# Parking only the sums' two parts in the down projections, with twelve parked and nine summed pairs per layer

## The chip, the cores and the metric

The kernel runs on one core of a Trainium2 chip. The metric is the device time of one execution in microseconds (us). TensorE is called PE here (PEld its weight loads), VectorE DVE, ScalarE ACT, GpSimd POOL and SyncE SP.

## The reference

Two post-norm layers on an input of 256 positions by 2048 features, all in 32-bit floats. Layer 0 mixes tokens with a gated MLP, layer 1 with latent attention; each mixer is followed by the same kind of gated MLP with a short convolution, and it is this MLP's last product that the change touches:

```python
def conv_ffn(x, w_up, conv_w, conv_b, w_down):
    h = x @ w_up                     # 2048 -> 2 * 5504
    ...                              # causal convolution of width 3 along the positions
    a, g = jnp.split(h, 2, axis=-1)
    return (jax.nn.silu(g) * a) @ w_down      # 5504 -> 2048: the down projection
...
    f = conv_ffn(x, ffn_w_up[i], ffn_conv_w[i], ffn_conv_b[i], ffn_w_down[i])
    x = layer_norm(ALPHA * x + f, ln_ffn_g[i], ln_ffn_b[i])
```

## The kernel before

**Products in parts.** PE multiplies a rounded type (`F32R`). So each operand is split into a high part `hi`, which ACT casts (line 125), and a low part `lo` = operand - `hi`, which DVE subtracts (line 128). A product is then three matmuls: high by high, low by high, high by low (`prod_b`).

**Units.** The down projection takes its 43 blocks of 128 rows of `w_down` in pairs, called units here (0 to 21; unit 21 is a single block). It does so twice, once for each half of the 2048 output columns, upwards in the first half and downwards in the second. A weight chunk of a unit is 128 partitions by 2 blocks of 1024 columns, thus 2048 columns in four pieces of 512. Each unit is of one of three kinds, written down by hand in `PLAN`:

- `e`, wide: `Banks.eight`, 8 products of 128 x 128 by 128 x 512, so 24 matmuls. The weights need two `big` tiles (high and low part).
- `s`, summed ("seven"): `Banks.seven`, 7 products, 21 matmuls, in the manner of Strassen's scheme. `_seven` forms four sums of the pieces (lines 135 and 138) and splits both the last three pieces (`wh`, `wl`, 1536 columns) and the sums (`th`, `tl`, 2048 columns). It takes five `big` tiles, one of which (`ts`, the sums themselves) is free once they are split. The activations need sums as well: `turn` (four small DVE instructions), two casts and two subtractions in `Acts.make`, in a room of their own, while two wide units share a room.
- `p`, parked: also 7 products, but the four tiles `wh`, `wl`, `th`, `tl` were made earlier, while the up projection ran, and stored in DRAM (`park`); `fetch` brings them back on POOL's DMA queue into four `side` tiles.

**Feeding.** `Feed` hands out the chunks in order. Before PE's work on a unit is issued, `next` has the following two (near the end three) split and two more loaded; `fetch` is called up to five units ahead (`LEAD`). Loads go through SP's queue, parking and fetching through POOL's. The tiles come from three pools of slots:

```python
SLOTS = {"big": 14, "raw": 3, "side": 6}
```

`raw` holds loaded weights until they are split, `big` split weights, activations, up to two residual tiles and four of the six tiles that hold the up projection's result (`act`), `side` the parked parts, the other two `act` tiles, and some activations of the second half. An instruction whose tile has no free slot waits until the users of an older tile are done.

**Parking.** `park` is a generator. `park_all` runs through the parked units in order, and the up projection takes one step of it (`next(jobs, None)`) behind two of the four chunks of most of its groups, 38 places in all. A parked unit takes four steps: load; split of the three plain pieces and two stores; the four additions; split of the sums and two stores.

**Ends.** After the last summed or parked unit of a half, `rest` and `fold` (DVE) take the banks of its sums into the residual; at the end of a half `piece` takes the other banks. The last three units (four in layer 1) are done bank by bank, interleaved with the layer norm.

The order of instructions on each engine follows from the program's order and the tiles' dependencies, arranged when the program is built.

Of the kernel before, what the change touches and what calls it, by code (L numbers as in the profile page):

```python
# [8 lines left out]
F32 = mybir.dt.float32  # L9
F32R = mybir.dt.float32r  # L10
BF16 = mybir.dt.bfloat16
AF = mybir.ActivationFunctionType
ALU = mybir.AluOpType
AX = mybir.AxisListType

P = 128
# [7 lines left out]
NF_FF = DFF // P  # L24
# [31 lines left out]
SLOTS = {"big": 14, "raw": 3, "side": 6}  # L56
# [4 lines left out]

PLAN = {NF_GM: ("0e 1e 2s 3e 4e 5s 6e 7e 8s 9e 10e 11s 12e 13e 14s 15e 16e 17s 18e 19e 20s 21e 22e 23e",
                "23e 22e 21e 20s 19e 18e 17s 16e 15e 14s 13e 12e 11s 10e 9e 8s 7e 6e 5s 4e 3e 2e 1e 0e"),
        NF_FF: ("0e 1p 2e 3s 4e 5e 6p 7e 8s 9e 10e 11p 12e 13s 14e 15p 16e 17s 18e 19s 20e 21e",
                "21e 20e 19p 18e 17s 16e 15p 14e 13s 12e 11p 10s 9e 8s 7p 6e 5s 4e 3e 2e 1e 0e")}
KINDS = {"e": "wide", "s": "seven", "p": "parked"}
FIRST = ((19, 1), (20, 0), (20, 2))
LEAD = 5
# [8 lines left out]
class Feed:  # L77
# [3 lines left out]
    def __init__(self, nc, pin, behind, order, pool, dram, chunks):  # L81
        self.pin, self.behind, self.order, self.sums = pin, behind, order, None
        self.nc, self.pool, self.dram, self.chunks = nc, pool, dram, chunks
        self.kept = {}
        self.raw, self.parts = {}, {}
        self.loaded = self.split = self.used = 0

    def _load(self):
        ap, cols, kind = self.chunks[self.loaded][:3]
        if kind == "parked":  # L90
            self.fetch(self.loaded)
            self.loaded += 1
            return
        t = self.pool.tile([P, 2048], F32, tag="raw", name=f"raw{self.loaded}", bufs=SLOTS["raw"])
        if len(ap.shape) == 3:
            self.behind(self.nc.sync.dma_start(t.rearrange("p (k c) -> p k c", k=ap.shape[1]), ap))
        else:
            step = 1024 if self.loaded < 3 else cols
            for o in range(0, cols, step):
                self.behind(self.nc.sync.dma_start(t[:, o : o + step], ap[:, o : o + step]))  # L100
        self.raw[self.loaded] = t
        self.loaded += 1

    def _split(self):
        i = self.split
        cols, kind = self.chunks[i][1:3]
        if kind == "parked":
            self.split += 1
            return
        raw = self.raw.pop(i)  # L110
        if kind == "seven":
            self.parts[i] = self._seven(i, raw)
            self.split += 1
            return
        hi = self.pool.tile([P, 2048], F32R, tag="big", name=f"wh{i}", bufs=SLOTS["big"])
        lo = self.pool.tile([P, 2048], F32R, tag="big", name=f"wl{i}", bufs=SLOTS["big"])
        step = 512 if i == 0 else cols if kind == "wide" and i > 2 else 1024 if cols == 2048 else cols // 2
        for o in range(0, cols, step):
            c = slice(o, o + step)
            self._cast(hi[:, c], lo[:, c], raw[:, c])  # L120
        self.parts[i] = (hi, lo)
        self.split += 1

    def _cast(self, hi, lo, raw):
# [23 lines left out]
    def park(self, i):  # L148

        nc, pin = self.nc, self.pin  # L150
        tile = lambda n, dt: self.pool.tile([P, 2048], dt, tag="side", name=f"{n}{i}", bufs=SLOTS["side"])
        add = lambda o, a, b: pin(nc.vector.tensor_tensor(o, a, b, ALU.add))
        self.kept[i] = kept = {}

        def store(n, t, cols):
            d = self.dram.tile([P, cols], F32, tag=f"kept{n}{i}", name=f"kept{n}{i}", bufs=1)
            pin(nc.gpsimd.dma_start(d, t[:, 0:cols].bitcast(F32)))
            kept[n] = d

        ap = self.chunks[i][0]  # L160
        raw = tile("praw", F32)
        pin(nc.gpsimd.dma_start(raw.rearrange("p (k c) -> p k c", k=ap.shape[1]), ap))
        yield
        for n, o, cols in (("w", 512, 1536), ("t", 0, 2048)):
            hi, lo = tile(f"p{n}h", F32R), tile(f"p{n}l", F32R)
            pin(nc.scalar.copy(hi[:, 0:cols], raw[:, o : o + cols]))
            pin(nc.vector.tensor_tensor(lo[:, 0:cols], raw[:, o : o + cols], hi[:, 0:cols].bitcast(F32), ALU.subtract))
            store(f"{n}h", hi, cols)
            store(f"{n}l", lo, cols)
            if n == "w":  # L170
                yield
                r = [raw[:, 512 * i : 512 * (i + 1)] for i in range(4)]
                add(r[1], r[1], r[0])
                add(r[0], r[0], r[2])
                add(r[2], r[2], r[1])
                add(r[3], r[3], r[2])
                yield

    def fetch(self, i):

        if i in self.parts:
            return
        got = self.parts[i] = []
        for n in ("wh", "wl", "th", "tl"):
            d = self.kept[i].pop(n)
            t = self.pool.tile([P, 2048], F32R, tag="side", name=f"f{n}{i}", bufs=SLOTS["side"])
            self.behind(self.nc.gpsimd.dma_start(t[:, 0 : d.shape[1]], d))
            got.append(t)
# [9 lines left out]
    def next(self, splits=2, loads=2):  # L198
        i = self.used
        self.ahead(i + 1 + splits + loads, i + 1 + splits)  # L200
        self.used += 1
        got = self.parts.pop(i)
        near = [j for j in range(i + 1, min(i + 1 + LEAD, len(self.chunks))) if self.chunks[j][2] == "parked"]
        if near and near[0] in self.kept:
            self.fetch(near[0])
        return got
# [3 lines left out]
def trunk(ctx: ExitStack, tc: tile.TileContext, x, xT, gm_in, gm_wout, ffn_up, ffn_dn,  # L210
# [344 lines left out]
    def boundary(ln, acc, end, tag, after):  # L555
# [15 lines left out]
        ln.piece(1, fs[1], acc[1][fs[1]])  # L571
        g = group(ln, tag)
        next(g)
        ln.put(0, 2)
        ln.scale(0, 3)
        ln.put(0, 3)
        ln.start(1)
        ln.scale(1, 0)
        next(g)
        ln.scale(1, 1)  # L580
        next(g)
        ln.put(1, 0)
        ln.scale(1, 2)
# [768 lines left out]
```

## Time and profile before

| | us |
|---|---|
| median of three runs | 2465.78 (2465.09 to 2467.02) |
| span of the profiled execution | 2464.6 |
| up projection and its boundary, layer 0 (780.0 to 1271.5) | 491.5 |
| down projection, layer 0 (1271.5 to 1493.9) | 222.4 |
| down projection, layer 1 (2232.2 to 2454.7) | 222.5 |
| last instructions behind it (2455.0 to 2464.6) | 9.6 |

The profile is of one execution on the chip. Its span runs from the first to the last instruction; the times of the runs hold a little more than that. A "busy" engine has an instruction in flight; matmuls overlap one another, so the time that one takes of PE is the distance between two starts, not its duration. A row of a group tells count, busy time, mean duration in ns of one, and the idle time ahead of it with what ended it. A row of the timeline tells start, duration, engine, line, what is written and read, and in brackets the engine's idle time just before and what ended it. Numbers of buffers are left out of tile names: `wh` is any unit's high part.

### The profile page before, as it was taken

What the parts mean: (1) busy time and instruction counts of PE and PEld (TensorE: products, weight loads), DVE (VectorE), ACT (ScalarE), POOL (GpSimd) and SP (SyncE); (2) the same over time, 40 slices, a digit from 0 to 9 for tenths busy, and PEclk for the clock granted to TensorE, in tenths of its full rate; (3) what the DMA queues carried; (4) which work ended last, traced back from release to release, by engine and by line L of the source; (5) the groups of instructions that cost most, each with busy time, mean ns of one, the idle gap of its engine ahead of it and who ended that gap; (6) DMA issues with size and microseconds to landing.
All of it is one profiled execution on the core that took longest, in us unless ns stands there. A gap on an engine that the chain in (4) does not pass through costs nothing. (4 is left out here: it accounts for less than half of the span.)

```text
span 2464.6 us, 32483 instructions
## 1 busy us (share of the span) xinstructions
PE 2458.1 (100%) x12494; PEld 2091.3 (85%) x12494; DVE 2054.7 (83%) x2734; ACT 1459.3 (59%) x1967; POOL 104.2 (4%) x202
## 2 busy tenths in 40 slices
PE   9999999999999999999999999999999999999999
PEld 7888888888888888888888888988888888888887
DVE  7999999989897788778777997867598787878798
ACT  6666665566565666656554566665565665555453
POOL 0000000000000000000001000000000000000000
PEclk9999999999999999999999999999999999999999
DMA  7555666656665778778868885544478787777885
GB/s 291 202 208 205 226 204 202 205 188 205 222 212 198 241 282 314 300 279 300 322 218 318 301 301 182 184 170 156 172 269 309 275 305 304 295 265 278 299 324 201
DMA packets 116428, 611.94 MB, mean 248 GB/s; under 512 B 10648, under 2 KB 10912, under 8 KB 75184
## 3 DMA queue, kind: packets, MB, share of 16 engines
q1 hardware_dynamic: 90128, 462.47, 52.9%
q0 software_dynamic: 26144, 147.39, 15.8%
q8 instruction: 98, 1.61, 0.3%
q14 instruction: 58, 0.48, 0.1%
HBM read 544.75 MB, written 65.06 MB: 247 GB/s over the span
## 5 line engine op out<-in xcount | busy, mean ns | idle before, releaser
L128 DVE TENSOR_TENSOR wl<-raw,wh 128x1024 fp32r<-128x1024 f32 (+4 forms) x645 | 958.4, 1501 | 169.5 <-ACT wh L125 124.0
L125 ACT CAST wh<-raw 128x1024 fp32r<-128x1024 f32 (+4 forms) x645 | 809.0, 1278 | 356.8 <-PE up L230 80.7
L230 PE MATMUL up<-xhl,wh 128*128 128x512 f32 x2624 | 611.4, 390 | 0.0
L230 PEld LDWEIGHTS up<-xhl,wh 128*128 128x128 f32 x2624 | 487.4, 188 | 97.8
L230 PEld LDWEIGHTS up<-xhl,wl 128*128 128x128 f32 x2624 | 325.8, 192 | 6.4
L230 PE MATMUL up<-xhl,wl 128*128 128x256 f32 x2624 | 328.1, 283 | 0.0
L125 ACT CAST th<-ts 128x1536 fp32r<-128x1536 f32 (+1 forms) x138 | 142.5, 1052 | 110.9 <-DVE ts L135 80.3
L230 PE MATMUL ub<-wh,xhl 128*128 128x512 f32 x576 | 179.5, 393 | 0.0
L128 DVE TENSOR_TENSOR tl<-ts,th 128x1536 fp32r<-128x1536 f32 (+1 forms) x138 | 163.2, 1221 | 10.4 <-PE dn_p L230 3.4
L230 PEld LDWEIGHTS ub<-wh,xhl 128*128 128x128 f32 x576 | 108.1, 188 | 24.2 <-issue 1.9
L230 PE MATMUL ub<-wl,xhl 128*128 128x512 f32 x288 | 112.1, 389 | 0.0
L135 DVE TENSOR_TENSOR ts<-ts,raw 128x512 f32<-128x512 f32 x138 | 95.1, 689 | 1.4
L135 DVE TENSOR_TENSOR ts<-raw 128x1024 f32<-128x1024 f32 x69 | 84.3, 1221 | 6.1 <-PE ub L230 3.8
L230 PE MATMUL mo<-wh,oT 128*128 128x512 f32 x256 | 82.5, 401 | 0.0
L230 PE MATMUL v_q<-wh,xhl 128*128 128x512 f32 x224 | 70.7, 391 | 0.3 <-ACT wh L125 0.3
L230 PEld LDWEIGHTS ub<-wl,xhl 128*128 128x128 f32 x288 | 54.1, 188 | 11.3
L230 PE MATMUL v_p<-wh,xhl 128*128 128x512 f32 x192 | 59.9, 389 | 0.0
L230 PEld LDWEIGHTS mo<-wh,oT 128*128 128x128 f32 x256 | 45.5, 189 | 7.1
L230 PEld LDWEIGHTS v_q<-wh,xhl 128*128 128x128 f32 x224 | 42.0, 188 | 10.5 <-ACT wh L125 1.9
L230 PE MATMUL mo<-wl,oT 128*128 128x512 f32 x128 | 50.1, 391 | 0.0
L724 ACT ACTIVATE lny<-lnt,lncol 128x128 f32<-128x128 f32 x96 | 36.6, 472 | 15.6 <-PE lnt L720 15.5
L388 DVE TENSOR_TENSOR h_0a<-up,lo_0a 128x256 f32<-128x256 f32 x41 | 17.2, 421 | 33.0 <-ACT lo_0a L386 33.0
(1838 smaller groups left out, 4338.4 us busy)
## 6 DMA issues: line engine op xcount, KB each, us to landing
raw<-in_ffn_up_dram SPq DMA_DIRECT2D x172, 1024.0 KB, 7.0
raw<-in_gm_in_dram SPq DMA_DIRECT2D x93, 1024.0 KB, 5.3
raw<-in_ffn_dn_dram SPq DMA_DIRECT2D x68, 1024.0 KB, 7.2
raw<-in_gm_wout_dram SPq DMA_DIRECT2D x48, 1024.0 KB, 5.3
praw<-in_ffn_dn_dram POOLq DMA_DIRECT2D x16, 1024.0 KB, 13.9
keptth<-pth POOLq DMA_DIRECT2D x16, 1024.0 KB, 8.1
kepttl<-ptl POOLq DMA_DIRECT2D x16, 1024.0 KB, 8.8
fth<-keptth POOLq DMA_DIRECT2D x16, 1024.0 KB, 9.4
```

The lines of the kernel that those rows point to most:

```text
L125: cast = self.nc.scalar.copy(hi, raw)
L128: self.nc.vector.tensor_tensor(lo, raw, hi.bitcast(F32), ALU.subtract)
L135: add = lambda o, a, b: self.nc.vector.tensor_tensor(o, a, b, ALU.add)
L230: recent[0] = nc.tensor.matmul(o, l, r, start=start, stop=stop, skip_group_check=True)
L388: nc.vector.tensor_tensor(h, acc[:, 0:S], lo, ALU.add)
L724: nc.scalar.activation(y[:, j], t[:, j * P : (j + 1) * P], AF.Identity, bias=lncol[:, o : o + 1], scale=lncol[:, g : g + 1])
```

## The change

A parked unit no longer stores and fetches the parts of its three plain pieces. `park` has three steps now: load, the four additions, and the split of the sums with two stores. `fetch` brings back two tiles instead of four. The plain pieces are loaded into a `raw` tile on SP's queue when the unit's turn comes, in two DMAs (512 columns and 1024 columns), and split like a wide unit's, 1536 columns at once, into two `big` tiles. `next` looks for the next parked unit that is not fetched yet.

`PLAN` changes for both layers' down projections: from eight parked and ten summed units per layer to twelve and nine, so 21 units of 7 products instead of 18. The plan of the gated MLP's output (`NF_GM`) stays.

```diff
-        NF_FF: ("0e 1p 2e 3s 4e 5e 6p 7e 8s 9e 10e 11p 12e 13s 14e 15p 16e 17s 18e 19s 20e 21e",
-                "21e 20e 19p 18e 17s 16e 15p 14e 13s 12e 11p 10s 9e 8s 7p 6e 5s 4e 3e 2e 1e 0e")}
+        NF_FF: ("0e 1p 2e 3s 4e 5p 6s 7e 8p 9e 10s 11e 12p 13s 14e 15p 16e 17s 18e 19p 20e 21e",
+                "21e 20e 19p 18s 17e 16p 15e 14s 13p 12e 11s 10p 9e 8p 7s 6e 5p 4e 3e 2e 1e 0e")}
...
     def _load(self):
         ap, cols, kind = self.chunks[self.loaded][:3]
+        t = self.pool.tile([P, 2048], F32, tag="raw", name=f"raw{self.loaded}", bufs=SLOTS["raw"])
         if kind == "parked":
+            self.behind(self.nc.sync.dma_start(t[:, 0:512], ap[:, 0, 512:1024]))
+            self.behind(self.nc.sync.dma_start(t[:, 512:1536], ap[:, 1]))
             self.fetch(self.loaded)
-            self.loaded += 1
-            return
...
     def _split(self):
...
-        if kind == "parked":
-            self.split += 1
-            return
...
+        cols = 1536 if kind == "parked" else cols
...
-        self.parts[i] = (hi, lo)
+        self.parts[i] = (hi, lo, *self.fetched.pop(i, ()))
...
     def park(self, i):
...
-        for n, o, cols in (("w", 512, 1536), ("t", 0, 2048)):
...
+        add(r[1], r[1], r[0])
+        add(r[0], r[0], r[2])
+        add(r[2], r[2], r[1])
+        add(r[3], r[3], r[2])
+        yield
+        hi, lo = tile("pth", F32R), tile("ptl", F32R)
+        pin(nc.scalar.copy(hi, raw))
+        pin(nc.vector.tensor_tensor(lo, raw, hi.bitcast(F32), ALU.subtract))
+        store("th", hi, 2048)
+        store("tl", lo, 2048)
...
     def fetch(self, i):
...
-        for n in ("wh", "wl", "th", "tl"):
+        for n in ("th", "tl"):
```

More of the change, by code (lines that the diff above doesn't have):

```diff
@@ L83, in __init__ @@
         self.nc, self.pool, self.dram, self.chunks = nc, pool, dram, chunks
-        self.kept = {}
+        self.kept, self.fetched = {}, {}
         self.raw, self.parts = {}, {}
@@ L89, in _load @@
         ap, cols, kind = self.chunks[self.loaded][:3]
+        t = self.pool.tile([P, 2048], F32, tag="raw", name=f"raw{self.loaded}", bufs=SLOTS["raw"])
         if kind == "parked":
+            self.behind(self.nc.sync.dma_start(t[:, 0:512], ap[:, 0, 512:1024]))
+            self.behind(self.nc.sync.dma_start(t[:, 512:1536], ap[:, 1]))
             self.fetch(self.loaded)
-            self.loaded += 1
-            return
-        t = self.pool.tile([P, 2048], F32, tag="raw", name=f"raw{self.loaded}", bufs=SLOTS["raw"])
-        if len(ap.shape) == 3:
+        elif len(ap.shape) == 3:
             self.behind(self.nc.sync.dma_start(t.rearrange("p (k c) -> p k c", k=ap.shape[1]), ap))
@@ L116, in _split @@
         lo = self.pool.tile([P, 2048], F32R, tag="big", name=f"wl{i}", bufs=SLOTS["big"])
-        step = 512 if i == 0 else cols if kind == "wide" and i > 2 else 1024 if cols == 2048 else cols // 2
+        cols = 1536 if kind == "parked" else cols
+        step = 512 if i == 0 else cols if kind == "parked" else cols if kind == "wide" and i > 2 else 1024 if cols == 2048 else cols // 2
         for o in range(0, cols, step):
@@ L163, in park @@
         yield
-        for n, o, cols in (("w", 512, 1536), ("t", 0, 2048)):
[L165 to L177, printed above, removed]
+        r = [raw[:, 512 * i : 512 * (i + 1)] for i in range(4)]
+        add(r[1], r[1], r[0])
[8 more added lines that the diff above has]
+        store("tl", lo, 2048)
     def fetch(self, i):
-        if i in self.parts:
+        if i in self.fetched:
             return
-        got = self.parts[i] = []
-        for n in ("wh", "wl", "th", "tl"):
+        got = self.fetched[i] = []
+        for n in ("th", "tl"):
             d = self.kept[i].pop(n)
@@ L202, in next @@
         got = self.parts.pop(i)
-        near = [j for j in range(i + 1, min(i + 1 + LEAD, len(self.chunks))) if self.chunks[j][2] == "parked"]
+        near = [j for j in range(i + 1, min(i + 1 + LEAD, len(self.chunks)))
+                if self.chunks[j][2] == "parked" and j not in self.fetched and j >= self.split]
         if near and near[0] in self.kept:
```

## The prediction

> **What bounds the kernel now.** I read the busy shares first, then the waits of PE, then the two down projections stretch by stretch, then single units in the timeline. The page's head:
>
> ```profile
> span 2464.6 us, 32483 instructions
> PE 2458.1 (100%) x12494; PEld 2091.3 (85%) x12494; DVE 2054.7 (83%) x2734; ACT 1459.3 (59%) x1967; POOL 104.2 (4%) x202
> ```
>
> PE covers the span. Its ends are modelled, so this alone does not say that it never starves; all that PE waited for in the list of waits is this:
>
> ```profile
> PE warm L230 <- POOL idle L281: 1.3, 1, 1.3
> PE fin L230 <- DVE dg L701: 0.3, 1, 0.3
> PE v_q L230 <- ACT wh L125: 0.3, 1, 0.3
> ```
>
> None of it lies in a down projection. In the timeline of PE the starts say what a matmul really takes (columns: start, duration, then the instruction; the first rows of units 18, 19 and 20 in the first half of layer 0):
>
> ```profile
> 1364.20 0.62 PE L230 MATMUL dn_q<-wh,dn018wx 128*128 128x512 f32 x2
> ...
> 1369.64 0.62 PE L230 MATMUL dn_q<-wh,dn019sx 128*128 128x512 f32 x2
> ...
> 1374.40 0.62 PE L230 MATMUL dn_q<-wh,dn018wx 128*128 128x512 f32 x2
> ```
>
> The wide unit 18 takes 1369.64 - 1364.20 = 5.44 us for its 24 matmuls, the summed unit 19 takes 4.76 us for 21: 0.227 us each, start to start. (Unit 20 reads the room named after 18.) A whole down projection has 8 + 10 units of 21, 24 of 24 and two half blocks of 12: 978 matmuls, 221.8 us at this rate. So PE sets the time, and a converted unit is worth 0.68 us if its inputs are on time.
>
> Whether they are is a matter of DVE. Stretches of layer 0 (up projection; units 0 to 17; unit 18 to the second half's 17; on to unit 5), three of layer 1, and the tail. Columns: length, busy time of PE, PEld, DVE, ACT, POOL, clock, DMA share, GB/s.
>
> ```profile
> 780.00:1271.50 491.50, 491.50 (x2801) 432.81 (x2800) 386.94 (x555) 298.12 (x440) 25.41 (x45) 1.00 0.74 273
> 1271.50:1361.40 89.90, 89.90 (x398) 74.46 (x397) 69.26 (x98) 46.68 (x52) 8.45 (x16) 1.00 0.86 316
> 1361.40:1400.20 38.80, 38.80 (x173) 32.13 (x172) 38.80 (x49) 18.81 (x19) 2.12 (x4) 1.00 0.76 266
> 1400.20:1458.30 58.10, 58.10 (x258) 48.08 (x258) 53.25 (x75) 36.29 (x39) 4.23 (x8) 1.00 0.92 339
> 2232.10:2321.90 89.80, 89.80 (x398) 74.36 (x397) 68.98 (x98) 46.57 (x52) 8.45 (x16) 1.00 0.85 317
> 2321.90:2360.70 38.80, 38.80 (x173) 32.14 (x172) 38.80 (x49) 18.84 (x19) 2.11 (x4) 1.00 0.71 262
> 2360.70:2418.80 58.10, 58.10 (x259) 48.08 (x257) 53.25 (x75) 35.62 (x37) 4.22 (x8) 1.00 0.93 342
> 2455.00:2464.60 9.60, 5.08 (x12) 1.75 (x10) 5.49 (x11) 0.29 (x1) 0.00 (x0) 0.95 0.29 109
> ```
>
> DVE has slack in the first stretch (69.3 of 89.9 us), none in the second (38.8 of 38.8) and little in the third (53.3 of 58.1). PE is the bound, and DVE is a hair behind it. From here both layers are alike, so I work out one and double it.
>
> DVE's prices, by its starts in the timeline (unit 14, then the activations and weights of unit 13), and two of its waits:
>
> ```profile
> 1339.07 2.29 DVE L128 TENSOR_TENSOR wl<-raw,wh 128x2048 fp32r<-128x2048 f32 x1 [4.96 <-PE dn_q L230]
> 1361.36 2.29 DVE L128 TENSOR_TENSOR wl<-raw,wh 128x2048 fp32r<-128x2048 f32 x1 [3.35 <-ACT wh L125]
> 1405.25 2.28 DVE L128 TENSOR_TENSOR wl<-raw,wh 128x2048 fp32r<-128x2048 f32 x1
> 1407.45 0.69 DVE L484 TENSOR_TENSOR dn015px<-dn015pt,dn015px 128x512 fp32r<-128x512 f32 x1
> ...
> 1409.26 0.29 DVE L291 TENSOR_TENSOR dn013st<-act 128x128 f32<-128x128 f32 x1
> 1409.46 0.29 DVE L292 TENSOR_TENSOR dn013st<-act 128x128 f32<-128x128 f32 x1
> ...
> 1410.67 1.22 DVE L135 TENSOR_TENSOR ts<-raw 128x1024 f32<-128x1024 f32 x1
> 1411.81 0.69 DVE L484 TENSOR_TENSOR dn013sx<-dn013st,dn013sx 128x512 fp32r<-128x512 f32 x1
> 1412.41 0.69 DVE L488 TENSOR_TENSOR dn013sx<-act,dn013sx 128x512 fp32r<-128x512 f32 x1
> 1413.01 0.69 DVE L135 TENSOR_TENSOR ts<-ts,raw 128x512 f32<-128x512 f32 x1
> 1413.61 1.76 DVE L128 TENSOR_TENSOR wl<-raw,wh 128x1536 fp32r<-128x1536 f32 x1
> 1415.28 0.69 DVE L135 TENSOR_TENSOR ts<-ts,raw 128x512 f32<-128x512 f32 x1
> ```
>
> Start to start: 2.20 us for 2048 columns, 1.67 for 1536, 1.14 for 1024, 0.60 for 512, 0.20 for 128. A wide unit costs DVE 2.20 + 0.60 (activations) = 2.80 us. A summed one costs 1.14 + 2 x 0.60 + 2 x 1.67 + 0.60 = 6.28 for weights and 4 x 0.20 + 2 x 0.60 = 2.00 for activations, 8.28 us in 4.76 us of PE. A parked one costs 2.00 now, and lets DVE catch up. The row at 1361.36 shows the margin: DVE ends at 1363.65, PE uses that tile 0.45 us into unit 18, at 1364.65 (matmuls 1 and 2 read only `wh`).
>
> **The change part by part.**
>
> PE: per layer 8 + 10 converted units become 12 + 9, three more. 3 x 3 matmuls x 0.227 = 2.04 us a layer, **-4.1 us** for both. The bank sums and the last units of each half stay as they are (the last converted unit is at the same place in both plans): nothing.
>
> DVE in the down projection, per layer: a parked unit now needs its plain blocks split in place, 1.67 us, so 3.67. Three wide units fewer (-8.4), one summed fewer (-8.3), 12 x 3.67 - 8 x 2.00 = +28.0: 11.3 us more, less up to 2.0 where a unit's activations are reused. By stretch:
> - Units 1 to 17 of the first half: before 4 parked, 4 summed, 9 wide; after 5, 5 and 7. 5 x 3.67 - 4 x 2.00 + 8.28 - 2 x 2.80 = +13.0 us, so 82.3 us of DVE in 89.9 - 2 x 0.68 = 88.5 us of PE. Its 20.6 us of idle time shrink to 6.2. Those were waits for a slot: 4.96 us at 1339.07 until PE released `big` tiles, 3.35 at 1361.36 behind a cast that had itself waited.
> - Unit 18 to the second half's third or fourth unit: 19 turns from summed to parked (-4.6), 19 comes again and now needs its plain split (+1.7), and 18 with 17 swap kinds (0). 2.9 us less, just where DVE has no idle time. But the summed one now comes a unit earlier; up to its place DVE has 38.8 - 2.9 - 2.8 = 33.1 us of work from 1361.4, so it ends near 1394.5. PE comes to that unit at 1395.5 (1364.2 plus 5.44 x 3 + 4.76 x 2 + 2.72 x 2 = 31.3 us) and to its last part some 2.5 us later: 3.5 us to spare on DVE alone.
> - The next eleven units: 3 parked, 4 summed, 4 wide become 4, 3 and 4: 4 x 3.67 + 3 x 8.28 - 3 x 2.00 - 4 x 8.28 = +0.4 us, and the unit ahead of them (16) turns from wide to parked, +0.9. Against 58.1 us, nothing.
>
> Slots: a parked unit takes two `big` tiles more. Any three neighbours of the new plan hold at most 8 (4 + 2 + 2), as many as two wide around a summed one hold before. But there are more such neighbourhoods, and a parked or summed unit's activations take a room of their own. What this costs no row shows. Lower bound -0.5 us a layer (the two gaps of PE among the last, interleaved units might close). Upper bound: DVE keeps all 20.6 us of its idle time in the first stretch, so that it lasts 82.3 + 20.6 = 102.9 instead of 88.5 us, +14.4. I take 0.5 us a layer, near the lower end, since PE's wait rows are nil with the same three-neighbour maximum in place: **+1.0 us**.
>
> ACT: a cast of 1536 columns for each parked unit, 1.48 us by the parking's own row below, 12 x 1.48 = 17.8 us before the fewer wide and summed casts are taken off. ACT is busy 46.7, 18.8 and 36.3 us of the three stretches, about half: nothing, unless a cast that waits for a slot holds those behind it; that is in the slot bound.
>
> Loads in the down projection, and what parking costs:
>
> ```profile
> raw<-in_ffn_dn_dram SPq DMA_DIRECT2D x14, 1024.0 KB, 7.6
> fth<-keptth POOLq DMA_DIRECT2D x4, 1024.0 KB, 9.8
> ftl<-kepttl POOLq DMA_DIRECT2D x4, 1024.0 KB, 13.2
> POOL fwh L187 <- PE dn_p L230: 256.0, 8, 67.4
> L166 ACT CAST pwh<-praw 128x1536 fp32r<-128x1536 f32 x8 | 11.8, 1480 | 7.6 <-DMA praw<-in_ffn_dn_dram 7.6
> L152 DVE TENSOR_TENSOR praw<-praw 128x512 f32<-128x512 f32 x32 | 22.0, 687 | 0.3
> L167 DVE TENSOR_TENSOR ptl<-praw,pth 128x2048 fp32r<-128x2048 f32 x8 | 18.3, 2285 | 0.3 <-ACT pth L166 0.3
> L167 DVE TENSOR_TENSOR pwl<-praw,pwh 128x1536 fp32r<-128x1536 f32 x8 | 14.0, 1752 | 6.1 <-ACT pwh L166 6.1
> ```
>
> Bytes per layer: 35 MB plain and 8 x 3584 KB fetched (64,512 KB) become 31 MB plain and 12 x (768 + 2048) KB (65,536 KB), 1.6% more where the DMA engines are 0.86 and 0.92 busy. Fetching two tiles per unit instead of four leaves room in the six `side` slots for the next pair, so POOL's wait for PE (256 us in eight) shrinks, and the burst of four becomes one of two. But the plain blocks now pass SP and its three `raw` slots: 44 loads instead of 36, in two pieces for a parked unit, 20 more issues a layer behind waits for a slot. A slot cycle is a load (7.6 us) and a hold of at most 6.3 (a summed unit): 13.9 us for three units of some 15 us. It fits by a little: nothing in the sum; a load of 12 us at each turn would not fit.
>
> The up projection: DVE's parking work goes from 22.0 + 18.3 + 14.0 = 54.3 us a layer to 1.5 x (22.0 + 18.3) = 60.5. That is 6.2 us more in a stretch where DVE is busy 386.9 of 491.5: hidden. The bytes stay (8 x 4608 KB = 12 x 3072 KB), POOL issues 36 instead of 40, the steps are 36 instead of 32 in 38 places, and a parked unit takes three `side` tiles instead of five: nothing.
>
> Sum: -4.1 + 1.0 = -3.1. The profiled execution spans 2464.6 us; the runs' median is 2465.78, 1.2 above. From the median: **2462.7 us**. A measurement of this kernel tells 0.2%, 4.9 us, from no change; the whole saving of PE is 0.17%. So what I forecast would be called the same.
>
> **The rivals.**
> - *DVE or the slots eat the saving.* PE waits some 2 us a layer, at the early summed unit of the second half or in the first stretch (93% DVE). For it: leads of a microsecond now. Against it: the 2.9 us of relief at the tightest place. 2465.8 us.
> - *Slower: the first stretch becomes DVE's.* At least 5.0 + 3.4 us of the idle time there is not lack of work but order: a split cannot start until PE frees a slot. If 12 us of the 20.6 stay where 6.2 are left, each layer gains 5.8 us: 2465.8 - 4.1 + 11.6 = 2473.3. It decides (over 0.2%) from 10.7 us of idle time that stay: 2 x (10.7 - 6.2) = 9.0 = 4.1 + 4.9. For it: raw loads that also come later. Against it: the plain split of a parked unit is short work that can fill such gaps.
> - *A long wait slows the clock.* In the tail PE is busy 5.1 of 9.6 us and the granted clock is 0.95, 1.00 elsewhere. One wait of some 4 us a layer would cost 8 us and 0.05 x 9.6 = 0.5 us of clock each: 2465.8 - 4.1 + 9 = 2470.7, just the bound. The Trainium skill, "TensorE: Matmul & The Clock Gate", section "Part 1: The HAM clock gate (the 'warmup' mystery)", says that after an idle window of about 3.4 us TensorE runs at half its clock until it has been busy for about as long. By that rule the estimate would be up to 1.7 us more for each such wait, 2472 to 2473. The trace agrees in kind: the clock falls in the one stretch with such idle time.
> - *More than the matmuls.* The gaps near the last units close and shorter bursts help: -4.1 - 1.0 = 2460.7.
>
> **How the numbers follow.** Forecast (2461.5 to 2464.5) 0.50; saving eaten (to 2469) 0.22; slower first stretch 0.15; clock 0.03; more than the matmuls 0.10. Faster by over 0.2%: 0.10. Slower: 0.15 + 0.03 = 0.18. Same: 0.72. The range from 2460.8 to 2470.0 leaves out about 0.08 below and 0.12 above. It takes in the lower bound of the slots; their upper bound (+28.8 us) lies outside.
>
> **What would show it.** Right: 969 matmuls a layer with the same 0.227 us; no new wait of PE in the down projections; DVE near 82 us in units 1 to 17, and some 3 us of idle time in the stretch that had none; POOL's waits on `dn_p` shorter; the up projection as long as before. Wrong: gaps between PE's starts at the second half's unit 18 or 16, or at summed units of the first half, released by ACT `wh` or by a raw load; a clock under 1.00 in a down projection.

## The result and the profile after

The changed kernel takes 2485.67 us (median of five runs, 2484.13 to 2487.05) against 2465.99 us of the kernel before on the same chip: a ratio of 1.008, 95% interval 1.007 to 1.0091. It is slower by 20 us, where I had forecast 2462.7 (2460.8 to 2470.0). The page's head, and the longest rows of PE's list of waits (total, times, longest; the rest of the list is 1.3 us at the program's start and rows of 0.5 us and less):

```profile
span 2483.2 us, 32569 instructions
...
PE 2460.0 (99%) x12476; PEld 2090.1 (84%) x12476; DVE 2089.2 (84%) x2794; ACT 1473.1 (59%) x1977; POOL 93.1 (4%) x178
```

```profile
PE dn_q L226 <- DVE h_0g L384: 3.4, 1, 3.4
PE dn_p L226 <- DVE h_0a L384: 3.1, 1, 3.1
PE dn_p L226 <- DVE h_1a L384: 3.1, 1, 3.1
PE dn_q L226 <- DVE h_1g L384: 2.6, 1, 2.6
PE dn_q L226 <- DVE dn010px L480: 1.5, 1, 1.5
PE dn_q L226 <- DVE dn110px L480: 1.4, 1, 1.4
```

(The changed kernel's line numbers are a few lower: `mm` is 226, the cast 123, the weights' subtract 126, `sum_halves` 382 and 384, the activations 479 to 484, `park` 150 to 170.) Before, no wait of PE lay in a down projection. Now there are two long ones in each layer, and they are not for weights: `h_` is the sum of the two halves of an up projection's bank, `h_0a` and `h_0g` of its last groups (`h_1a` and `h_1g` in layer 1). The last three of the seven products of the down projection's unit 1 go into PSUM banks that the up projection has used until then; the fifth and the sixth wait long.

The stretches of layer 0 as in the prediction (up projection; units 0 to 17; unit 18 to the second half's 17; the next eleven units), moved with the work. Columns: length, busy time of PE, PEld, DVE, ACT, POOL, clock, DMA share, GB/s.

```profile
779.30:1270.80 491.50, 491.50 (x2801) 432.86 (x2800) 389.55 (x566) 291.79 (x433) 24.10 (x41) 1.00 0.72 269
1270.80:1368.90 98.10, 91.36 (x392) 74.48 (x391) 84.49 (x117) 57.68 (x64) 5.29 (x10) 0.97 0.83 307
1368.90:1407.70 38.80, 38.80 (x172) 32.10 (x172) 36.27 (x44) 20.13 (x20) 2.11 (x4) 1.00 0.75 264
1407.70:1466.80 59.10, 57.64 (x253) 47.13 (x252) 56.98 (x80) 37.81 (x41) 3.17 (x6) 1.00 0.96 352
```

The up projection is as long as before. The first stretch takes 98.1 us instead of 89.9, the last 59.1 instead of 58.1. In numbers from PE's starts, for each stage (from the first start of its first matmul to the first start of the next stage's):

| profiled execution | up, layer 0 | down, layer 0 | up, layer 1 | down, layer 1 |
|---|---|---|---|---|
| before | 461.48 | 242.84 | 461.44 | 222.02 |
| after | 461.50 | 252.35 | 461.82 | 231.00 |

(Layer 0's down projection is counted to the first `mkv` matmul, so it has the boundary behind it in it; layer 1's to the start of its last matmul.) Down costs 9.5 and 9.0 us more, of 18.6 us between the two spans. Per layer PE has 969 matmuls instead of 978 (-2.04 us) and stands still, over its usual 0.227 us from start to start, for 11.6 and 11.4 us instead of 0.1 and 0.5: 9.5 and 8.6 at unit 1, 1.7 and 1.6 at unit 10 of the second half, the rest in short waits at its units 16, 13 and 2.

**What happens at unit 1.** PE's timeline (start, duration, instruction, and in brackets the idle time ahead of it):

```profile
1278.94 0.39 PE L226 MATMUL dn_q<-ftl,dn01px 128*128 128x512 f32 x1
1282.69 0.70 PE L226 MATMUL dn_q<-fth,dn01px 128*128 128x512 f32 x2 [3.36 <-DVE h_0g L384]
1283.23 0.39 PE L226 MATMUL dn_q<-ftl,dn01px 128*128 128x512 f32 x1
1286.71 1.19 PE L226 MATMUL dn_p<-fth,dn01px 128*128 128x512 f32 x2 [3.10 <-DVE h_0a L384]
1287.70 0.63 PE L226 MATMUL dn_p<-ftl,dn01px 128*128 128x512 f32 x1
1288.13 1.05 PE L226 MATMUL dn_q<-wh,dn00wx 128*128 128x512 f32 x2
...
1290.32 1.19 PE L226 MATMUL dn_p<-fth,dn01px 128*128 128x512 f32 x2 [0.28 <-DVE h_0g L384]
```

The fetched parts (`fth`, `ftl`) are there; what is missing is the bank. The two waits take 3.5 and 3.3 us of PE, and after the second one the starts are 0.43 us apart (1287.70 to 1288.13), half pace, for some 4 us. Over all 14 us the granted clock is 0.76; in the second row, which begins within the second wait, it is 0.50:

```profile
1278.00:1292.00 14.00, 7.26 (x21) 4.83 (x21) 12.48 (x21) 9.56 (x15) 0.20 (x1) 0.76 0.40 152
1284.67:1291.49 6.82, 4.50 (x10) 3.17 (x11) 6.82 (x14) 5.08 (x8) 0.00 (x0) 0.50 0.11 41
```

That is the half clock of the Trainium skill, "TensorE: Matmul & The Clock Gate", "Part 1: The HAM clock gate (the 'warmup' mystery)"; the trace agrees with it in the pace, with 0.43 us for 0.227 behind a stretch of 7.8 us of which PE was idle 6.5. The rule of the Trainium skill that the prediction gives asks for an idle window of about 3.4 us; in that the traces differ from it, since two kernels below have the half clock behind waits of 1.6 and 1.8 us (last section).

ACT's and DVE's timelines say why the bank is late:

```profile
1270.37 1.48 ACT L123 CAST wh<-raw 128x1536 fp32r<-128x1536 f32 x1 [4.13 <-DMA raw<-in_ffn_dn_dram]
1277.58 1.91 ACT L123 CAST wh<-raw 128x2048 fp32r<-128x2048 f32 x1 [5.73 <-DMA raw<-in_ffn_dn_dram]
1279.39 0.60 ACT L903 ACTIVATE c_0a<-h_0a,cst 128x256 f32<-128x256 f32 x1
1279.89 0.35 ACT L382 COPY lo_0g<-up 128x256 f32<-128x256 f32 x1
...
1285.36 0.42 ACT L920 ACTIVATE s<-c_0g 128x256 f32<-128x256 f32 x1 [1.57 <-DVE c_0g L906]
1285.68 0.35 ACT L382 COPY lo_0a<-up 128x256 f32<-128x256 f32 x1
```

```profile
1279.52 2.29 DVE L126 TENSOR_TENSOR wl<-raw,wh 128x2048 fp32r<-128x2048 f32 x1 [5.88 <-ACT wh L123]
1281.73 0.48 DVE L904 SCALAR_TENSOR_TENSOR c_0a<-h_0a,cst,c_0a 128x255 f32<-128x255 f32 x1
1282.12 0.42 DVE L384 TENSOR_TENSOR h_0g<-up,lo_0g 128x256 f32<-128x256 f32 x1
...
1286.15 0.42 DVE L384 TENSOR_TENSOR h_0a<-up,lo_0a 128x256 f32<-128x256 f32 x1
```

ACT works in the order that was set when the program was built. In it the casts of units 1 and 2 stand ahead of the last copies out of the up projection's banks. Both casts wait for their raw loads, 4.13 and 5.73 us, with `lo_0g` (0.35 us) queued behind them. `lo_0g` comes at 1279.89, DVE, which had itself waited 5.88 us for the second cast, adds `h_0g` at 1282.12, and PE starts at 1282.69. The second bank inherits the delay: its copy `lo_0a` stands on ACT behind the activation `s`, which needs the convolution `c_0g` of the first, so `h_0a` comes at 1286.15 and PE starts at 1286.71. Before, unit 1 needed no raw load at all, and unit 2's was early.

The loads are late because of what else is under way. The issues between 1248 and 1282 us (KB each, median us from issue to landing), after, and then the row of before in the same stretch:

```profile
raw<-in_ffn_dn_dram SPq DMA_DIRECT2D x4, 1024.0 KB, 11.8
fth<-keptth POOLq DMA_DIRECT2D x2, 1024.0 KB, 14.3
ftl<-kepttl POOLq DMA_DIRECT2D x2, 1024.0 KB, 14.3
keptth<-pth POOLq DMA_DIRECT2D x1, 1024.0 KB, 5.9
kepttl<-ptl POOLq DMA_DIRECT2D x1, 1024.0 KB, 11.4
...
raw<-in_ffn_dn_dram SPq DMA_DIRECT2D x1, 512.0 KB, 12.9
```

```profile
raw<-in_ffn_dn_dram SPq DMA_DIRECT2D x6, 1024.0 KB, 5.2
```

The last parking's two stores, the first unit's fetch and the second unit's fetch, 6 MB on POOL's queue, share the DMA engines with the raw loads of units 1 and 2; 11.5 MB move in these 34 us, 6.0 before. Before, the parking had ended at 1206 us, its last store had landed at 1215, and no transfer of POOL ran between 1235 and 1279 us. With 36 steps in 38 places instead of 32, and three steps to a unit, parking's last store is now issued 48 us later, right at the seam.

### The profile page after: what moved, and what is told of

It reads as the page before. It is cut to its first block, busy times and chain, and to the rows that moved or that the text cites. A ratio compares the mean times of both kernels' runs of the same rounds, so it can differ in the third digit from the quotient of the medians.

```text
span 2483.2 us, 32569 instructions
## 1 busy us (share of the span) xinstructions
PE 2460.0 (99%) x12476; PEld 2090.1 (84%) x12476; DVE 2089.2 (84%) x2794; ACT 1473.1 (59%) x1977; POOL 93.1 (4%) x178
## 5 line engine op out<-in xcount | busy, mean ns | idle before, releaser
L126 DVE TENSOR_TENSOR wl<-raw,wh 128x1024 fp32r<-128x1024 f32 (+4 forms) x661 | 981.7, 1502 | 183.2 <-ACT wh L123 132.2
L123 ACT CAST wh<-raw 128x1024 fp32r<-128x1024 f32 (+4 forms) x661 | 827.8, 1278 | 394.5 <-PE up L226 80.1
L150 DVE TENSOR_TENSOR praw<-praw 128x512 f32<-128x512 f32 x96 | 66.0, 687 | 12.4 <-DMA praw<-in_ffn_dn_dram 11.8
L170 DVE TENSOR_TENSOR ptl<-praw,pth 128x2048 fp32r<-128x2048 f32 x24 | 54.9, 2287 | 3.5 <-ACT pth L169 3.4
L169 ACT CAST pth<-praw 128x2048 fp32r<-128x2048 f32 x24 | 45.8, 1910 | 11.3 <-DVE praw L150 11.3
```

Source lines behind the costliest of these rows:

```text
L123: cast = self.nc.scalar.copy(hi, raw)
L126: self.nc.vector.tensor_tensor(lo, raw, hi.bitcast(F32), ALU.subtract)
L169: pin(nc.scalar.copy(hi, raw))
L170: pin(nc.vector.tensor_tensor(lo, raw, hi.bitcast(F32), ALU.subtract))
```

## The experiments

Theory A, from these rows: parking that ends late slows the raw loads, and ACT's order makes the up projection's last banks wait for them. Theory B, the strongest rival of the prediction: DVE or the slots can't keep up with 12 x 3.67 us of parked units, and unit 1 is only where it shows first. Theory C: the fetched parts come too late. All results in one table (times of the runs; stages from PE's starts in the profiled execution). The stages are of one execution, and its time is not the median. It lies 3.5 us above it in e2_act_order and 1.3 in e11_activations_first, and below it by 6.6 in e7_load_ahead_plan, 2.9 in e1_early_parking, 1.8 in e10_activation_first and 1.6 in e9_load_before_stores_plan. Small differences between stages of two kernels are to be read with that in mind.

| kernel | median us | ratio to before, 95% | up 0 | down 0 | up 1 | down 1 |
|---|---|---|---|---|---|---|
| e1_early_parking | 2492.83 | 1.0117 (1.0101 to 1.0134) | 474.28 | 242.92 | 471.96 | 221.34 |
| e2_act_order | 2474.00 | 1.0035 (1.0022 to 1.0049) | 461.46 | 250.80 | 462.09 | 224.37 |
| e3_old_plan_two_parts | 2470.45 | 1.0020 (1.0010 to 1.0029) | 461.46 | 244.86 | 461.45 | 223.51 |
| e5_early_and_order | 2500.43 | 1.0141 (1.0125 to 1.0156) | 478.78 | 246.46 | 472.27 | 223.23 |
| e6_load_ahead | 2494.83 | 1.0122 (1.0107 to 1.0137) | 476.06 | 243.50 | 474.58 | 222.13 |
| e7_load_ahead_plan | 2496.23 | 1.0127 (1.0110 to 1.0144) | 472.51 | 243.22 | 472.22 | 223.67 |
| e8_load_before_stores | 2466.13 | 1.0005 (0.9996 to 1.0014) | 461.50 | 243.35 | 461.44 | 221.38 |
| e9_load_before_stores_plan | 2476.12 | 1.0044 (1.0031 to 1.0056) | 461.50 | 248.21 | 461.49 | 225.46 |
| e10_activation_first | 2465.51 | 0.9999 (0.9991 to 1.0008) | 461.50 | 241.81 | 461.45 | 221.55 |
| e11_activations_first | 2464.88 | 0.9997 (0.9988 to 1.0006) | 461.50 | 242.81 | 461.45 | 222.01 |

**Parking ends earlier.**

```diff
-                if gi > 1 and c in (1, 2) and gi + c > 3:
+                if gi > 1 and (c in (1, 2) and gi + c > 3 or c == 3 and gi % 2):
```

> The changed kernel, but with a third place for a parking step in every second group of the up projection, so that the last parked unit is stored some 80 us before the down projection instead of 6 us. Theory A (crowded loads, blocked order): the last parking's two stores and the first two fetches share the DMA engines with the raw loads of units 1 and 2, which land after 13 and 15 us instead of 5; their casts stand in ACT's queue ahead of a copy that frees a PSUM bank, so PE waits at unit 1. Without the stores the loads land in 5 to 9 us, PE's gaps at unit 1 (3.5 + 3.3 us, then half clock) fall below 1 us, and the time goes from 2485.7 to about 2466 (2464 to 2469). Theory B (DVE and slots, the rival of the prediction): the first stretch is DVE's; earlier parking moves nothing there, 2484 to 2487. Theory C (the fetched parts themselves are late): earlier parking lets the first fetch start earlier, so about 2466 too.

Down falls to 242.92 and 221.34 us, with the same plan and the same work on DVE: the waits at unit 1 are gone and PE loses only 2.2 and 1.8 us a layer, 1.9 and 1.6 of it at unit 10. That speaks against B. But the up projections get 12.8 and 10.5 us longer. DVE's and PE's waits there:

```profile
DVE praw L150 <- DMA praw<-in_ffn_dn_dram: 82.6, 16, 8.9
```

```profile
PE up L226 <- DVE wl L126: 11.6, 8, 2.8
```

The additions of a parked pair now stand on DVE too close behind their load; the up projection's own subtractions queue up behind them.

**ACT's order at the seam.** Parking as in the changed kernel; the casts of units 1 to 3 are ordered on ACT behind the last copies from the up projection's banks.

```diff
+        if self.split in self.first and self.copies is not None:
+            self.order(cast, self.copies)
...
-        nc.scalar.copy(lo, acc[:, S : 2 * S])
+        feed.copies = nc.scalar.copy(lo, acc[:, S : 2 * S])
...
+        feed.first = [next(i for i in parked if i > feed.used) + j for j in range(3)]
```

> The changed kernel, but on ACT the casts of units 1 to 3 are ordered behind the up projection's copies that precede them in the program; loads, parking and fetches are as before. Theory A: the loads still take 13 to 15 us, but the banks are free in time, so the two gaps at unit 1 go; what is left is unit 2's weights some 0.5 us late and whatever follows from that: 2466 to 2470. Theory B: nothing gained, 2484 to 2487. Theory C: the parts land when they did, nothing gained, 2484 to 2487.

The loads are as late as before, but the copies no longer wait for them (ACT's timeline):

```profile
1275.29 0.35 ACT L385 COPY lo_0a<-up 128x256 f32<-128x256 f32 x1
1276.21 0.60 ACT L906 ACTIVATE c_0a<-h_0a,cst 128x256 f32<-128x256 f32 x1 [0.57 <-DVE h_0a L387]
1276.72 0.35 ACT L385 COPY lo_0g<-up 128x256 f32<-128x256 f32 x1
1277.85 1.91 ACT L124 CAST wh<-raw 128x2048 fp32r<-128x2048 f32 x1 [0.78 <-DMA raw<-in_ffn_dn_dram]
```

`lo_0g` comes 3.2 us earlier and PE no longer waits for a bank, so C falls (the parts were there in time). The time drops by 11.7 us. What stays: PE waits at unit 3 (1.5 and 1.2 us) and above all at 18 (4.1 us in layer 0, some 1.7 of it the half clock behind the wait, and 1.3 in layer 1), besides 2.0 and 1.6 at the second half's 10. Both halves of theory A are needed for the wait at unit 1, since either cure takes it away; but down is 7.9 and 3.0 us longer than with early parking.

**Two parts with the old plan.** The changed kernel with the plan of before (8 parked, 10 summed), thus 24 steps of parking.

> One part of the change alone: a parked unit keeps only the sums' two parts, its plain blocks are split in place, but the plan is the old one (8 parked, 10 summed). PE has no matmul fewer. Theory A: 24 parking steps end far ahead of the seam, so the loads of units 1 and 2 meet only the fetches; waits at unit 1 under 2 us a layer; 2466 to 2470. Theory B: DVE has 8 x 1.67 = 13 us a layer more, the first stretch 82 of 90 us: PE waits spread over units 3 to 17, 2472 to 2486.

4.8 us more than before, with no wait of any size at unit 1, but short ones at other parked units (1.0 us at 15 in layer 1, 1.0 around 7 in both), and the end 1.3 us longer, for a reason that no run shows. This is what splitting the plain pieces in place costs by itself. The three converted units more are not in it.

**Both cures together.** The edits of the first two kernels.

> Both edits together, early parking and ACT's order. Theory A: unit 1 has no gap at all; what remains of the loss is the 1.6 us a layer at unit 10 of the second half; 2464 to 2466, level with the kernel before or a little under it. Theory B: 2484 to 2487.

2500.43 us. The up projections stay long for the reason seen in the first (DVE waits 88.3 us for parking's loads), and down is 3.5 and 1.9 us longer than with early parking alone. Of that, 0.8 and 1.2 us are a wait at unit 18, which of all kernels only the two with the forced order have: that is what the order costs where nothing is left to cure. But 2.1 of the 3.5 us are not its price: at the second half's 10 PE waits 1.8 us here and 1.7 with early parking alone, and only here the clock is at 0.50 for 3.4 us behind it. The wait at unit 3, which the kernel with the order alone has, is gone here; that one is the late loads'.

**The load a step ahead.** The load of the next parked pair is issued with the split of this one, and places are chosen so that parking ends in group 18 of 21.

```diff
-        for i in [i for i in parked if feed.used < i < until]:
-            yield from feed.park(i)
+        each = [feed.park(i) for i in parked if feed.used < i < until]
+        next(each[0])
+        yield
+        for n, unit in enumerate(each):
+            next(unit)
             yield
+            next(unit, None)
+            if n + 1 < len(each):
+                next(each[n + 1])
+            yield
...
-                if gi > 1 and c in (1, 2) and gi + c > 3:
+                if c in (1, 2) and (gi % 4 and gi > 2 or gi == c == 2):
```

> The changed kernel with parking done earlier, but without the early parking's own flaw: the load of the next parked unit is issued with the split of this one, so that its additions come three chunks (16 us) later and DVE does not stand in front of a load; two steps a unit, in 12 of the groups, the last stores about 55 us before the down projection. Theory A: up projections as long as before (461 us, not 472 to 474 as with the first early parking), no gap at unit 1, down projections as with the first early parking (222 and 221 us between the first and last matmul, with the 1.7 us at unit 10 of the second half still in them): 2464 to 2466, within 0.2% of the kernel before. If DVE or the slots were the cause (theory B), 2475 or more.

Down is good again (243.50 and 222.13), but my expectation for the up projections was missed: they are 14.6 and 13.1 us longer.

```profile
DVE praw L150 <- DMA praw<-in_ffn_dn_dram: 87.2, 14, 10.0
```

On POOL's queue the load still stands behind the two stores of the pair before, as in the changed kernel. They wait for ACT and DVE, so the load is issued right after the second of them and lands some 15 us later.

**The same, and the plan around 10 changed** to look at the other wait, `11s 10e 9p 8p` for `11s 10p 9e 8p` in the second half.

> The same, and in the second half units 10, 9 and 8 change kinds (10 wide, 9 and 8 parked, as many of each kind): the wait at unit 10 comes from DVE's work for a summed unit directly followed by a parked one's activations and split, so with a wide unit there it should go. Theory A: the full saving of PE less some tenths, 2461 to 2463.5. If the wait only moves on to units 9 or 8, 2464 to 2466, as the other.

The wait at that place shrinks to 0.6 and 0.4 us, and 1.4 and 2.5 us appear some 27 us later, at unit 5. Nothing gained.

**The load ahead of the stores.** As e6_load_ahead, at the same places, but the load of the next pair is issued with the additions of this one, so ahead of its stores on POOL's queue.

```diff
         for n, unit in enumerate(each):
+            if n + 1 < len(each):
+                next(each[n + 1])
             next(unit)
             yield
             next(unit, None)
-            if n + 1 < len(each):
-                next(each[n + 1])
             yield
```

> The load of the next parked pair is issued together with the additions of this one, ahead of this one's stores on POOL's queue and a whole group (some 22 us) ahead of its own additions; the last parking ends in group 18 of the up stage, two groups before its end. If the loss of the two earlier-parking kernels came only from loads standing behind stores, DVE should wait under 10 us in all for parking loads, the up stages last 461.5 to 464 us, the down stages 242.9 to 243.5 and 221.3 to 222.2 us as in the other kernels that park early, and the time is 2464 to 2469 us, at or just under the kernel before. If it came from the parking's work being denser on DVE (an additional 6.9 us per pair), the up stages stay 10 us longer and the time is 2485 to 2497 us.

2466.13 us, the time of before. The up projections are back at 461.50 and 461.44. DVE's group of the additions (last column: idle time ahead of them), the raw loads between 1248 and 1282 us, and all that PE waits for in the down projections:

```profile
L150 DVE TENSOR_TENSOR praw<-praw 128x512 f32<-128x512 f32 x96 | 65.6, 683 | 0.1
```

```profile
raw<-in_ffn_dn_dram SPq DMA_DIRECT2D x4, 1024.0 KB, 5.3
raw<-in_ffn_dn_dram SPq DMA_DIRECT2D x2, 512.0 KB, 5.6
```

```profile
PE dn_q L226 <- DVE dn010px L480: 1.8, 1, 1.8
...
PE dn_q L226 <- DVE dn110px L480: 1.3, 1, 1.3
```

Against e6_load_ahead one thing moved, and 87.2 us of waiting became nothing: the loss of e6_load_ahead in the up projection was the load's place in POOL's queue, not the work. (e1_early_parking has the same wait, 82.6 us, at other places; it was not run with the load moved.) Against the changed kernel the parking's order and places moved, and 19.5 us went: theory A's loss, 18.1 us at unit 1, whole. What is left is the wait at unit 10. It takes 2.1 and 1.5 us, of the 2.04 us a layer that PE saves.

**A third plan,** `10e 9p 8e 7s 6p 5p` behind the same parking. (In the text on record for it and for the next kernel, "converted" means a wide unit.)

> As the last kernel, and the second half's units 10 to 5 become converted, parked, converted, summed, parked, parked, so that a converted unit's weights stand no longer just ahead of the first activation of 10. If the 1.5 to 2 us that PE waits at 10 come from that order on DVE, the down stages get some 1.5 us shorter each, 241.5 and 220 us, and the time is 3 us under the last kernel's; if DVE lacks time in this stretch as a whole, the wait moves on to a unit behind and nothing is gained.

Slower by 10 us: PE now waits at 9 for that unit's activations, 7.2 us over its pace in layer 0 (the half clock included) and 4.0 in layer 1.

**The activations of 10 first.** In the timeline of DVE of e8_load_before_stores, the weights of unit 9 (the first row, 2.2 us) stand ahead of the activations of 10 for which PE waits (the second):

```profile
1434.43 2.28 DVE L126 TENSOR_TENSOR wl<-raw,wh 128x2048 fp32r<-128x2048 f32 x1
1436.64 0.68 DVE L480 TENSOR_TENSOR dn010px<-dn010pt,dn010px 128x512 fp32r<-128x512 f32 x1
```

The next two kernels order these weights behind the activations; the first at this place alone, the second behind every parked and summed unit.

```diff
+        if self.split in self.held:
+            self.order(sub, self.held[self.split])
...
+                if (u, kind) == (10, "parked") and self.n_k == NF_FF:
+                    feed.held[feed.split + 1] = sub
```

> The kernel that issues the load ahead of the stores, and on DVE the weights' subtract of the converted unit behind 10 (2.21 us) is ordered behind the activations' subtract of 10. If that one place is what holds PE there, its wait of 2.17 and 1.64 us shrinks to 0.6 us or less, nothing else moves, the down stages last some 241.7 and 219.9 us and the time is 2462 to 2463.5 us, 0.1 per cent under the kernel before. If DVE has no time to spare in this stretch, the wait comes back a unit or two later (at 9 or 8) and the time stays at 2465 to 2466.5 us.

> The same order for every parked and summed unit of the down projections: the weights of the unit behind it come after its activations' subtract on DVE. If the order at 10 is one case of a general one, nothing is gained over the kernel with the one place (2462 to 2463.5 us). If it forces waits elsewhere, because activations have to wait for a room that PE frees and now hold weights behind them, new waits of PE at units of the first half appear and the time is 2466 to 2475 us.

2465.51 and 2464.88 us, neither to be told from before. PE's waits in the down projections of the first:

```profile
PE dn_q L229 <- DVE dn12wx L490: 1.2, 1, 1.2
PE dn_q L229 <- DVE dn010px L483: 0.5, 1, 0.5
```

In layer 0 the wait shrinks by 1.4 us and down is 1.0 us shorter than before; in layer 1 it shrinks by 1.2, and 1.4 us over PE's pace stand at unit 2 of the second half, 38 us later. So DVE's order made the wait at 10. That it comes back at 2 because DVE has too little room in the last stretch is not shown: the changed kernel and e6_load_ahead have 0.8 and 0.7 us at unit 2 beside their wait at 10, and e8_load_before_stores has none. The second kernel waits at unit 2 as well (1.3 us) and, 0.7 us, at unit 1 of layer 0 for `h_0g`.

## Why the prediction was wrong

**The step that failed** is the seam between up and down. I wrote of the up projection "the steps are 36 instead of 32 in 38 places" and "nothing", and of the loads "nothing in the sum". Both were counted within a stage. I didn't ask where the parking ends (its last store landed at 1215 us before, at 1266 after), which transfers then lie beside the first raw loads (5.2 us became 11.8 and more), nor that unit 1 had needed no raw load and now does. The room that I counted as a gain, "leaves room in the six `side` slots for the next pair", let the second unit's fetch start at 1257 us, right there. I had written that a load of 12 us would not fit, without looking for what could make one. And I covered ACT by its busy share, "about half: nothing, unless a cast that waits for a slot holds those behind it": a cast that waits for a load does the same, and what it held was the release of a bank. Cost: 9.5 and 8.6 us of PE, taken away whole by e8_load_before_stores.

**The clock rival** came nearest in kind: a wait of some 4 us a layer with the clock lowered behind it, 2470.7, and 2472 to 2473 by the rule of the Trainium skill. It had a chance of 0.03. There are two such waits a layer and the slow pace behind them is half, so it is 18 us instead of 8 to 9.

**What held**, read where the seam is repaired (e8_load_before_stores; units 0 to 17, unit 18 to 17, and on as in the prediction):

```profile
1271.50:1360.00 88.50, 88.50 (x392) 73.32 (x391) 82.09 (x115) 53.85 (x60) 5.29 (x10) 1.00 0.85 308
1360.00:1398.80 38.80, 38.80 (x173) 32.15 (x172) 36.33 (x44) 20.21 (x20) 2.11 (x4) 1.00 0.77 270
1398.80:1458.30 59.50, 57.60 (x253) 46.92 (x252) 55.88 (x81) 36.67 (x38) 3.18 (x6) 1.00 0.96 346
```

- PE: 969 matmuls at the same pace. The first stretch lasts 88.5 us, as worked out, and three converted units more a layer are worth 4.3 us (2466.13 against 2470.45 of the old plan with two parts), 4.1 forecast. Two things differ between these two kernels, the plan and the parking's places, and only the sum is measured.
- DVE in the first stretch: 82.09 us busy, 82.3 forecast, and PE waits for nothing there, so the slower rival "the first stretch becomes DVE's" fell.
- The second stretch: 2.5 us of idle time on DVE where there had been none, 2.9 forecast.
- Slots: no run singles out the 0.5 us a layer that I took. Outside unit 10 PE stands still for 0.4 and 0.3 us, at units 16 and 13; whether slots are behind that stays open. The two gaps among the last units, which I counted as up to 0.5 us in each layer, are in layer 1 alone; layer 0 had 0.1.
- POOL's waits for `dn_p` should have got shorter. In the changed kernel a single one did: the longest took 25.4 us and sixteen 281.6, where the longest before took 67.4 and eight 256.0. Their total did not.

**What was mis-sized**: the last stretch. I put down +1.3 us of DVE "against 58.1 us, nothing". DVE is busy 55.88 of 59.5 us there, 2.6 more than before, and PE waits 2.1 and 1.5 us at unit 10. This is the rival "DVE or the slots eat the saving", some 2 us a layer and 2465.8 us, right in size with the seam repaired (2466.13), at another place than the two I named. The in-place split costs 4.8 us with the old plan (3.5 in the two down columns, 1.3 at the end) where I had 1.0. So even without the seam the change would have given nothing measurable.

## What to carry to other kernels

Where a change moves work into an earlier stage, look at the end of that stage: which transfers are then still under way, and what on each in-order engine stands behind the first instruction that waits for them. A small copy that frees a bank, queued behind a cast that waits for a load, stops the engine that sets the time. An idle share of an engine doesn't cover that; its order has to be read. And on a queue of transfers, put the load that is wanted soon ahead of stores that have to wait for their data.

## What was not expected of the hardware

A raw load of 1 MB, 5.2 us from issue to landing with no transfer of POOL's queue beside it, took 11.8 us at the median with 6 MB of parking's transfers beside it, and one of 512 KB took 12.9.

Where the granted clock falls to 0.50 in these traces, other than at a program's very end, it does so for 3.41 or 6.83 us. At unit 1 it falls 1.1 us into the second wait. Behind the first wait the starts were still 0.31 and 0.23 us apart, so the 0.9 us of work between the two waits did not keep the clock up. Shorter waits were enough elsewhere. In e2_act_order PE waits 1.59 us at unit 18, a little behind a wait of 0.42, and then has half the clock:

```profile
1369.07:1372.48 3.41, 3.41 (x9) 2.65 (x10) 2.65 (x4) 3.37 (x3) 0.00 (x0) 0.50 0.41 154
```

In e5_early_and_order 1.79 us at unit 10 did the same, while at that place 1.66 us in e1_early_parking and 1.8 us in e8_load_before_stores left the clock at 1.00. So a wait of under 2 us can cost another 1.7, and its length alone does not tell whether it will.
